# Mean and eps of the head sums on VectorE, the recurrence's elementwise chain in halves, seven temporaries

## The chip, the cores and the metric

The kernel runs on one core of one Trainium2 chip. The metric is the device time of one execution in microseconds (us). Its engines go by the profile's short names: PE is TensorE's matmul part and PEld its weight load, DVE is VectorE, ACT is ScalarE, POOL is GpSimd, and SP issues the DMAs.

## The reference

Two layers of one kind ("A": gated linear attention, grouped attention, a feed-forward part) are followed by two layers of another ("B"), on one sequence of 256 tokens of 1024 features, all in fp32. The change touches the head norms of both kinds and, in B, the gated recurrence beside the attention:

```python
for i in range(DEPTH):                                   # DEPTH = 2
    x = x + 0.5 * swiglu_ffn(rms_norm_2(x, ffn1_norm[i]), ffn1_w_in[i], ffn1_w_out[i])
    h = rms_norm_2(x, mix_norm[i])
    rx, rgate, q, k, v, f_logit, ga, gb = jnp.split(h @ w_in[i], split_idx, axis=-1)
    rx = causal_dwconv(rx, conv_w[i], conv_b[i])
    # rg_lru: r = sigmoid(rx @ w_a + b_a); ig = sigmoid(rx @ w_x + b_x)
    #   log_a = -8 * r * softplus(-lam); a = exp(log_a)
    #   u = sqrt(-expm1(2 * log_a)) * (ig * rx); y_t = a_t * y_(t-1) + u_t
    ya = (rg_lru(rx, ...) * jax.nn.gelu(rgate)) @ w_rnn_out[i]
    # q and k: rms_norm over each head of 128 features, then causal attention
    yb = forgetting_attention(q, k, v, f_logit, ...) @ w_attn_out[i]
    merged = jax.nn.sigmoid(ga + mb_a) * ya + jax.nn.sigmoid(gb + mb_b) * yb
    x = x + merged @ w_o[i]
    ...                                                  # second swiglu_ffn, gated input
```

## The kernel before

**Weights.** Every weight comes from memory once, as raw tiles of 128x1024 floats. ACT copies each tile into a rounded tile `hi` (L254) and DVE takes the rest into `lo` (L255). A product is three matmuls for each block: hi by the high part of x, hi by its low part, lo by the high part. `gemm_fm` (L292 to L294, 128x256 each) gives features by tokens, `gemm_tm` (L319 to L321, 128x512 each) tokens by features. In layer A a weight tile is split in two pieces of 128x512.

**Accumulators.** A product goes to a PSUM tile `acc` of 128x512; three buffers hold these in turn, and a buffer is free when the engine that reads the product out (ACT or DVE) has done so. A 128x512 accumulator of `gemm_fm` with 1024 input features takes 48 matmuls.

**The part of layer B around the change**, function `mixer_b`. First come the products for the recurrence's input (after the convolution `xc`, in a buffer named b3), v, f and the recurrence's output gate `rg` (buffer oh). Then small matmuls give r (b0) and ig (b1) through sigmoids with a bias (L1039), 128x256 at a time. The elementwise chain works on tiles of 128x2048: r times a factor for each feature (L1040), Tanh (L1042) and Exp (L1043) on ACT, ig times xc on POOL (L1044), a square (L1046) and a product (L1047) on DVE, a root on ACT (L1048), a product (L1049) and the recurrence itself as a scan (L1051) on DVE. The scan is one over all eight feature blocks; a memset of the first column of r (L1050) cuts them apart. The result times Gelu of rg (L1054, L1055) is split into high and low parts (L368, L369).

**Heads.** The q and k products (`heads`, four accumulators of 128x512 for q and four for k) are read out by ACT into a temporary `t` (L1064). Their squares (L471, ACT) are summed for each head (L472, DVE); `rstd` takes mean and eps (L336) and the power (L337) on POOL. DVE multiplies (L1070), PE transposes into PSUM (L1073), and ACT copies out to the q and k tiles (L1074), which take over the buffers b0 and b1 when the recurrence has no more use of them. Layer A has its own heads with the same `rstd` and a rotation behind it (L703, L712 to L724).

**Gates.** The product with w_gab follows in the same queue of PE: accumulators acc2211, acc2218, acc2225 and on in the first B layer. DVE reads each out (L383, times a row of norms) into sig_a (b2) and sig_b (b3), which are free again when the chain is through with `th` and `xc`.

**Order.** Nothing sets the order of instructions by hand. A scheduler lays out each engine's queue ahead of time from priorities: `urgent(offset, floor)` raises those of the weight splits and of the read-out of accumulators (`epilogue`). An engine takes its queue strictly in that order. Which of a pool's buffers a tile gets follows from the order in which the scheduler sees them come free. In B layers the temporaries `t` have six buffers (`T_BUFS_B`).

Of the kernel before, what the change touches and what calls it, by code (L numbers as in the profile page):

```python
# [14 lines left out]
AF = mybir.ActivationFunctionType  # L15
ALU = mybir.AluOpType
AX = mybir.AxisListType

P = 128
D = 1024  # L20
S = 256
KB = 8
HID = 2816
NHB = HID // P
EPS = 1e-6
# [5 lines left out]
SPLIT_B = 1024  # L31
EPI_PRIO = 5000
T_BUFS_A = {"t": 6, "px": 2, "sq": 2, "sy": 1, "dg": 2, "e": 1, "g": 2}
T_BUFS_B = {"t": 6, "px": 2, "sq": 1, "dg": 2}
START_PRIO = 20000
HOLD_MIX = (1, 3)
HOLD_FFN = (0, 2)
# [146 lines left out]
class Net:  # L184
# [148 lines left out]
    def rstd(self, ssq, n, cols):  # L333

        nc = self.nc
        nc.gpsimd.tensor_scalar(ssq, ssq, 1.0 / n, EPS, ALU.mult, ALU.add)  # L336
        nc.gpsimd.tensor_tensor(ssq, ssq, self.expo[:, :cols], ALU.pow)  # L337

    def rstd_of_halves(self, ssq, tag):
# [568 lines left out]
def layer_b(net, i, nrm, px, hT, following):  # L908
# [12 lines left out]
    with ExitStack() as cx:  # L921
        ms = mixer_b(net, i, cx, after)
        px = ple_input(net, a["pT_2"][i])
        nrm = NormT(net, hT, col(2))
        net.gemm_fm(ms, a["w_o"][i], net.add_scaled(hT, 1.0, nrm.blocks), tail=True)
# [20 lines left out]
def mixer_b(net, i, cx, nrm):  # L946
    nc, a, tc = net.nc, net.a, net.tc
# [3 lines left out]
    fl = lambda t: t.rearrange("p a b -> p (a b)")  # L951
# [3 lines left out]
    cc = lambda k, j: cols[:, 8 * k + j:8 * k + j + 1]  # L955
# [3 lines left out]
    sp = p1.tile([P, 16], F32, tag="sp", name=net.name("sp"))  # L959
# [41 lines left out]
    xc = big("b3")  # L1001
# [22 lines left out]
    rg = big("oh")  # L1024
# [3 lines left out]
    r, ig = big("b0"), big("b1")  # L1028
    for w, dst in ((0, r), (1, ig)):
        hi, lo = net.weight(a["rg_w"][i, w])  # L1030
        for fp in range(4):
            ps = net.pm.tile([P, 2, S], F32, tag="pm", name=net.name("rg"))
            for c in range(2):
                f = 2 * fp + c
                cs = slice(f * P, (f + 1) * P)
                nc.tensor.matmul(ps[:, c], lhsT=hi[:, cs], rhs=xch[:, f], start=True, stop=False)
                nc.tensor.matmul(ps[:, c], lhsT=hi[:, cs], rhs=xcl[:, f], start=False, stop=False)
                nc.tensor.matmul(ps[:, c], lhsT=lo[:, cs], rhs=xch[:, f], start=False, stop=True)
                nc.scalar.activation(dst[:, f], ps[:, c], AF.Sigmoid, bias=cc(5 + w, f))  # L1039
    nc.vector.tensor_tensor(r, r, sp[:, 0:8].unsqueeze(2).to_broadcast([P, KB, S]), ALU.mult)  # L1040
    th = big("b2")
    nc.scalar.activation(fl(th), fl(r), AF.Tanh)  # L1042
    nc.scalar.activation(fl(r), fl(r), AF.Exp, scale=-1.0)  # L1043
    nc.gpsimd.tensor_tensor(fl(ig), fl(ig), fl(xc), ALU.mult)  # L1044

    nc.vector.tensor_tensor(fl(xc), fl(r), fl(r), ALU.mult)  # L1046
    nc.vector.scalar_tensor_tensor(fl(th), fl(xc), 1.0, fl(th), ALU.add, ALU.mult)  # L1047
    nc.scalar.activation(fl(th), fl(th), AF.Sqrt)  # L1048
    nc.vector.tensor_tensor(fl(ig), fl(ig), fl(th), ALU.mult)  # L1049
    nc.gpsimd.memset(r[:, :, 0:1], 0.0)  # L1050
    nc.vector.tensor_tensor_scan(fl(xc), fl(r), fl(ig), 0.0, ALU.mult, ALU.add)  # L1051

    y_h, y_l = big("yh", F32R), big("yl", F32R)
    nc.scalar.activation(fl(rg), fl(rg), AF.Gelu_apprx_tanh)  # L1054
    nc.vector.tensor_tensor(fl(rg), fl(rg), fl(xc), ALU.mult)  # L1055
    for j in range(4):
        net.split_fm(blk(rg, j), y_h, y_l, 2 * j)

# [37 lines left out]
def _build(tc, a, out):  # L1096
    with ExitStack() as ctx:
# [11 lines left out]
        net.hp = hp  # L1109
        net.temporaries(ctx, T_BUFS_B)  # L1110
        net.split = SPLIT_B
# [153 lines left out]
```

## Time and profile before

| what | value |
|---|---|
| median of 3 runs | 2320.55 us (2308.11 to 2325.23) |
| profiled execution | 2315.75 us |
| span of its instructions | 2313.9 us |
| granted clock, mean | 0.991 |
| A layers, B layers | about 0 to 980 us, then to the end |
| busy: PE, DVE, ACT, POOL | 98%, 69%, 58%, 19% |

The rows below come from the profiled execution alone; 1.85 us lie around its span. "Idle before" names the engine's pause ahead of a row and what ended it. The durations of neighbouring rows of one engine overlap by about 0.1 us, so a row's share of a queue is read from its start to the next row's start.

### The profile page before, as it was taken

To read this page: it belongs to the slowest core of one execution; us is meant where nothing else is said; L and a number is where in the kernel's file an instruction comes from. 1 tells how busy PE (TensorE), PEld (TensorE's weight loads), DVE (VectorE), ACT (ScalarE), POOL (GpSimd) and SP (SyncE) were. 2 spreads that over 40 slices of the span, in tenths; PEclk is the share of its full clock that TensorE was granted. 3 is DMA by queue.
4 is the path that set the end of the run, shared out by engine and by line. 5 is a ranking of instruction groups with operands and counts; after the bars stand their busy time and mean duration, and the time that the engine had idled before them with its cause. 6 is when DMAs were issued, how large, how long until landed. Compare 5 with 4: busy or idle time off the path is not lost.

```text
span 2313.9 us, 42188 instructions
## 1 busy us (share of the span) xinstructions
PE 2262.1 (98%) x16892; PEld 2147.9 (93%) x16892; DVE 1602.1 (69%) x2133; ACT 1333.4 (58%) x2105; POOL 442.6 (19%) x443
## 2 busy tenths in 40 slices
PE   7999999998999999999999999999999999999997
PEld 6899899878899998799999899999999998999997
DVE  7876765588867765766586967655765677766655
ACT  6875554467764654554457765444644567755444
POOL 6222211063302110311001302110110104011101
PEclk9999999999999999999999999999999999999999
DMA  7445566554456666466665546666566655456663
GB/s 252 150 155 159 186 208 190 182 164 156 147 163 183 206 195 186 151 198 186 188 184 185 162 141 198 189 189 184 180 188 186 180 186 174 147 175 191 185 188 94
DMA packets 117102, 411.53 MB, mean 178 GB/s; under 512 B 14114, under 2 KB 16546, under 8 KB 116906
## 3 DMA queue, kind: packets, MB, share of 16 engines
q1 hardware_dynamic: 116906, 408.84, 57.5%
q8 instruction: 133, 2.18, 0.4%
q14 instruction: 63, 0.52, 0.1%
HBM read 407.74 MB, written 1.05 MB: 177 GB/s over the span
## 4 chain that ended last, share of the span: by engine, by line
PE 88%; DVE 4%; POOL 2%; ACT 2%; issue 2%; DMA 1%; SPq 0%; DVEq 0%; POOLq 0%; ACTq 0%
PE acc L292 22%; PE acc L293 22%; PE acc L294 22%; PE acc L319 5%; PE acc L320 5%; PE acc L321 5%; DVE lo L255 1%; ACT hi L254 1%; PE sc L586 1%; PE po L597 1%; PE gs L894 1%; POOL t L717 1%; PE sc L610 0%; POOL hg L78 0%; POOL tab L693 0%
## 5 line engine op out<-in xcount | busy, mean ns | idle before, releaser
L255 DVE TENSOR_TENSOR lo<-raw,hi 128x512 fp32r<-128x512 f32 (+1 forms) x1062 | 984.5, 954 | 424.4 <-ACT hi L254 422.4
L254 ACT ACTIVATE hi<-raw 128x512 fp32r<-128x512 f32 (+1 forms) x1062 | 824.0, 808 | 733.9 <-PE acc L293 386.3
L292 PE MATMUL acc<-xTh,hi 128*128 128x256 f32 x3296 | 923.5, 281 | 11.1 <-ACT t L1064 8.5
L293 PE MATMUL acc<-xTl,hi 128*128 128x256 f32 x3296 | 926.1, 281 | 1.0 <-DVE xTl L133 0.8
L294 PE MATMUL acc<-xTh,lo 128*128 128x256 f32 x3296 | 923.5, 280 | 0.0
L292 PEld LDWEIGHTS acc<-xTh,hi 128*128 128x128 f32 x3296 | 621.8, 189 | 13.3 <-ACT t L1064 8.9
L294 PEld LDWEIGHTS acc<-xTh,lo 128*128 128x128 f32 x3296 | 627.0, 190 | 0.4
L293 PEld LDWEIGHTS acc<-xTl,hi 128*128 128x128 f32 x3296 | 624.2, 189 | 2.8 <-DVE xTl L133 1.7
L400 POOL TENSOR_TENSOR t<-t,R 128x512 f32<-128x512 f32 x66 | 105.6, 1600 | 602.3 <-ACT t L398 602.3
L292 PE MATMUL acc<-hh,hi 128*128 128x256 f32 x704 | 197.8, 281 | 0.0
L293 PE MATMUL acc<-hl,hi 128*128 128x256 f32 x704 | 197.8, 281 | 0.0
L294 PE MATMUL acc<-hh,lo 128*128 128x256 f32 x704 | 197.8, 281 | 0.0
L319 PE MATMUL acc<-hi,xTh 128*128 128x512 f32 x416 | 164.6, 401 | 6.4 <-ACT hi L254 6.2
L320 PE MATMUL acc<-lo,xTh 128*128 128x512 f32 x416 | 166.6, 401 | 1.5 <-DVE lo L255 1.4
L321 PE MATMUL acc<-hi,xTl 128*128 128x512 f32 x416 | 165.4, 399 | 0.8 <-DVE xTl L355 0.8
L294 PEld LDWEIGHTS acc<-hh,lo 128*128 128x128 f32 x704 | 134.4, 191 | 0.0
L293 PEld LDWEIGHTS acc<-hl,hi 128*128 128x128 f32 x704 | 132.9, 189 | 0.0
L292 PEld LDWEIGHTS acc<-hh,hi 128*128 128x128 f32 x704 | 132.1, 188 | 0.0
L319 PEld LDWEIGHTS acc<-hi,xTh 128*128 128x128 f32 x416 | 79.1, 191 | 22.7 <-ACT hi L254 6.1
L320 PEld LDWEIGHTS acc<-lo,xTh 128*128 128x128 f32 x416 | 79.1, 190 | 19.0 <-DVE lo L255 3.3
L321 PEld LDWEIGHTS acc<-hi,xTl 128*128 128x128 f32 x416 | 79.2, 190 | 17.8 <-DVE xTl L355 1.5
L383 DVE TENSOR_TENSOR t<-acc,R 128x512 f32<-128x512 f32 (+1 forms) x84 | 56.8, 676 | 41.1 <-PE acc L294 41.1
(321 smaller groups left out, 3236.0 us busy)
## 6 DMA issues: line engine op xcount, KB each, us to landing
raw<-ffn_w_in SPq DMA_DIRECT2D x176, 512.0 KB, 3.7
raw<-w_ffn_in SPq DMA_DIRECT2D x88, 512.0 KB, 4.3
raw<-ffn_w_out SPq DMA_DIRECT2D x88, 512.0 KB, 4.3
raw<-w_ffn_out SPq DMA_DIRECT2D x44, 512.0 KB, 4.3
raw<-w_gate SPq DMA_DIRECT2D x32, 512.0 KB, 4.0
raw<-w_gab SPq DMA_DIRECT2D x32, 512.0 KB, 3.6
raw<-w_gqk SPq DMA_DIRECT2D x16, 512.0 KB, 3.9
raw<-w_gv SPq DMA_DIRECT2D x16, 512.0 KB, 3.3
```

The costliest lines, as they stand in the source:

```text
L254: nc.scalar.activation(hi[:, cs], raw[:, cs], AF.Copy)
L255: nc.vector.tensor_tensor(lo[:, cs], raw[:, cs], hi.bitcast(F32)[:, cs], ALU.subtract)
L292: nc.tensor.matmul(o, lhsT=hi[:, cs], rhs=xh[:, kb], start=kb == 0, stop=False)
L293: nc.tensor.matmul(o, lhsT=hi[:, cs], rhs=xl[:, kb], start=False, stop=False)
L294: nc.tensor.matmul(o, lhsT=lo[:, cs], rhs=xh[:, kb], start=False, stop=kb == nkb - 1)
L319: nc.tensor.matmul(o, lhsT=xh[:, kb, ts], rhs=hi[:, cs], start=kb == 0, stop=False)
L320: nc.tensor.matmul(o, lhsT=xh[:, kb, ts], rhs=lo[:, cs], start=False, stop=False)
L321: nc.tensor.matmul(o, lhsT=xl[:, kb, ts], rhs=hi[:, cs], start=False, stop=kb == 2 * n - 1)
L383: self.nc.vector.tensor_tensor(v(out), v(acc), r, ALU.mult)
L400: nc.gpsimd.tensor_tensor(tb, tb, nrm.R.unsqueeze(1).to_broadcast([P, 2, S]), ALU.mult)
L586: nc.tensor.matmul(sc[:, j], lhsT=q_t[:, hp * 2 + j, tt * P:(tt + 1) * P], rhs=k_t[:, hp // 2], start=True, stop=True)
L597: nc.tensor.matmul(out[:, j], lhsT=v(jt, hp // 2), rhs=p_t[:, jt], start=jt == 0, stop=jt == 1)
```

## The change

`rstd` takes the mean and eps on DVE and leaves only the power to POOL; all head norms, of A and of B, use it. The recurrence's chain is made in two halves of 128x1024 (four feature blocks each), step by step; the product ig times xc goes from POOL to DVE; the sigmoids of r and ig get the priority that read-outs have. The Gelu and the product behind the scan are in halves too. Temporaries in B layers have seven buffers.

```diff
--- before.py
+++ after.py
@@ -31,7 +31,7 @@
 SPLIT_B = 1024
 EPI_PRIO = 5000
 T_BUFS_A = {"t": 6, "px": 2, "sq": 2, "sy": 1, "dg": 2, "e": 1, "g": 2}
-T_BUFS_B = {"t": 6, "px": 2, "sq": 1, "dg": 2}
+T_BUFS_B = {"t": 7, "px": 2, "sq": 1, "dg": 2}
 START_PRIO = 20000
 HOLD_MIX = (1, 3)
 HOLD_FFN = (0, 2)
@@ -333,7 +333,7 @@
     def rstd(self, ssq, n, cols):
 
         nc = self.nc
-        nc.gpsimd.tensor_scalar(ssq, ssq, 1.0 / n, EPS, ALU.mult, ALU.add)
+        nc.vector.tensor_scalar(ssq, ssq, 1.0 / n, EPS, ALU.mult, ALU.add)
         nc.gpsimd.tensor_tensor(ssq, ssq, self.expo[:, :cols], ALU.pow)
 
     def rstd_of_halves(self, ssq, tag):
@@ -1036,23 +1036,27 @@
                 nc.tensor.matmul(ps[:, c], lhsT=hi[:, cs], rhs=xch[:, f], start=True, stop=False)
                 nc.tensor.matmul(ps[:, c], lhsT=hi[:, cs], rhs=xcl[:, f], start=False, stop=False)
                 nc.tensor.matmul(ps[:, c], lhsT=lo[:, cs], rhs=xch[:, f], start=False, stop=True)
-                nc.scalar.activation(dst[:, f], ps[:, c], AF.Sigmoid, bias=cc(5 + w, f))
-    nc.vector.tensor_tensor(r, r, sp[:, 0:8].unsqueeze(2).to_broadcast([P, KB, S]), ALU.mult)
+                with net.urgent(EPI_PRIO, 100):
+                    nc.scalar.activation(dst[:, f], ps[:, c], AF.Sigmoid, bias=cc(5 + w, f))
     th = big("b2")
-    nc.scalar.activation(fl(th), fl(r), AF.Tanh)
-    nc.scalar.activation(fl(r), fl(r), AF.Exp, scale=-1.0)
-    nc.gpsimd.tensor_tensor(fl(ig), fl(ig), fl(xc), ALU.mult)
-
-    nc.vector.tensor_tensor(fl(xc), fl(r), fl(r), ALU.mult)
-    nc.vector.scalar_tensor_tensor(fl(th), fl(xc), 1.0, fl(th), ALU.add, ALU.mult)
-    nc.scalar.activation(fl(th), fl(th), AF.Sqrt)
-    nc.vector.tensor_tensor(fl(ig), fl(ig), fl(th), ALU.mult)
-    nc.gpsimd.memset(r[:, :, 0:1], 0.0)
-    nc.vector.tensor_tensor_scan(fl(xc), fl(r), fl(ig), 0.0, ALU.mult, ALU.add)
+
+    halves = lambda step: [step(slice(4 * q, 4 * q + 4)) for q in range(2)]
+    v, s_ = nc.vector, nc.scalar
+    halves(lambda h: v.tensor_tensor(r[:, h], r[:, h], sp[:, h].unsqueeze(2).to_broadcast([P, 4, S]), ALU.mult))
+    halves(lambda h: s_.activation(fl(th[:, h]), fl(r[:, h]), AF.Tanh))
+    halves(lambda h: s_.activation(fl(r[:, h]), fl(r[:, h]), AF.Exp, scale=-1.0))
+    halves(lambda h: v.tensor_tensor(fl(ig[:, h]), fl(ig[:, h]), fl(xc[:, h]), ALU.mult))
+
+    halves(lambda h: v.tensor_tensor(fl(xc[:, h]), fl(r[:, h]), fl(r[:, h]), ALU.mult))
+    halves(lambda h: v.scalar_tensor_tensor(fl(th[:, h]), fl(xc[:, h]), 1.0, fl(th[:, h]), ALU.add, ALU.mult))
+    halves(lambda h: s_.activation(fl(th[:, h]), fl(th[:, h]), AF.Sqrt))
+    halves(lambda h: nc.gpsimd.memset(r[:, h, 0:1], 0.0))
+    halves(lambda h: v.tensor_tensor(fl(ig[:, h]), fl(ig[:, h]), fl(th[:, h]), ALU.mult))
+    halves(lambda h: v.tensor_tensor_scan(fl(xc[:, h]), fl(r[:, h]), fl(ig[:, h]), 0.0, ALU.mult, ALU.add))
 
     y_h, y_l = big("yh", F32R), big("yl", F32R)
-    nc.scalar.activation(fl(rg), fl(rg), AF.Gelu_apprx_tanh)
-    nc.vector.tensor_tensor(fl(rg), fl(rg), fl(xc), ALU.mult)
+    halves(lambda h: s_.activation(fl(rg[:, h]), fl(rg[:, h]), AF.Gelu_apprx_tanh))
+    halves(lambda h: v.tensor_tensor(fl(rg[:, h]), fl(rg[:, h]), fl(xc[:, h]), ALU.mult))
     for j in range(4):
         net.split_fm(blk(rg, j), y_h, y_l, 2 * j)
```

Line numbers behind L1039 move by up to four in the changed kernel: the head read-out L1064 becomes L1068, L1070 becomes L1074, L1051 becomes L1055, L1055 becomes L1059. Three places show what the scheduler makes of it, in the first B layer. DVE first, around the read-out of the first gate accumulator, acc2211, before:

```order
L472 TENSOR_REDUCE hss2154_14183<-sq2155_14184 128x4
L255 TENSOR_TENSOR lo2231_14548<-raw2229_14546,hi2230_14547 128x1024
L1049 TENSOR_TENSOR b12047_13685<-b12047_13685,b22062_13771 128x2048
L255 TENSOR_TENSOR lo2235_14580<-raw2233_14578,hi2234_14579 128x1024
L1070 TENSOR_TENSOR t2156_14189<-t2153_14181,hss2154_14183 128x512
L255 TENSOR_TENSOR lo2238_14610<-raw2236_14608,hi2237_14609 128x1024
L383 TENSOR_TENSOR b22209_14389<-acc2211_14391,R1686_10775 128x512
L1051 SCALAR_TENSOR_TENSOR b31945_12935<-b02046_13684,b12047_13685 128x2048
L383 TENSOR_TENSOR b22209_14389<-acc2218_14453,R1686_10775 128x512
```

And in the changed kernel:

```order
L1051 SCALAR_TENSOR_TENSOR b22062_13770<-b31945_12935,b22062_13770 128x1024
L255 TENSOR_TENSOR lo2228_14530<-raw2226_14528,hi2227_14529 128x1024
L472 TENSOR_REDUCE hss2135_14111<-sq2136_14112 128x4
L255 TENSOR_TENSOR lo2231_14560<-raw2229_14558,hi2230_14559 128x1024
L1054 TENSOR_TENSOR b12047_13685<-b12047_13685,b22062_13770 128x1024
L336 TENSOR_SCALAR hss2135_14111<-hss2135_14111 128x4
L255 TENSOR_TENSOR lo2235_14592<-raw2233_14590,hi2234_14591 128x1024
L383 TENSOR_TENSOR b22209_14401<-acc2211_14403,R1686_10775 128x512
L1055 SCALAR_TENSOR_TENSOR b31945_12935<-b02046_13684,b12047_13685 128x1024
L1074 TENSOR_TENSOR t2137_14117<-t2134_14109,hss2135_14111 128x512
```

The read-out of acc2211 (L383) stood behind the eighth lo tile of the gates (lo2238) and ahead of the whole scan. Now it stands behind the seventh (lo2235) and ahead of the scan's second half; the first half of the scan, with the Gelu product and two splits of its result, is already behind it in the queue.

PE's queue, from the last matmuls of acc2211 to the first of acc2218, with the engines that each waits for, before:

```order
L293 MATMUL acc2211_14391<-xTl1685_10774,hi2216_14423 128x256
L294 MATMUL acc2211_14391<-xTh1684_10773,lo2217_14424 128x256
L292 MATMUL acc2218_14453<-xTh1684_10773,hi2220_14455 128x256 [waits Activation_49]
L293 MATMUL acc2218_14453<-xTl1685_10774,hi2220_14455 128x256
L294 MATMUL acc2218_14453<-xTh1684_10773,lo2221_14456 128x256 [waits DVE_49]
```

And in the changed kernel:

```order
L293 MATMUL acc2211_14403<-xTl1685_10774,hi2216_14435 128x256
L294 MATMUL acc2211_14403<-xTh1684_10773,lo2217_14436 128x256
L292 MATMUL acc2218_14465<-xTh1684_10773,hi2220_14467 128x256 [waits DVE_49,PE_49]
L293 MATMUL acc2218_14465<-xTl1685_10774,hi2220_14467 128x256
L294 MATMUL acc2218_14465<-xTh1684_10773,lo2221_14468 128x256
```

The first matmul of acc2218 waited for ACT, which had its hi tile to write. It now waits for DVE and for PE itself: acc2218 lies in the buffer that acc2211 has just filled, and can start only behind its read-out by DVE. The second B layer has the same with its first two gate accumulators; no other two neighbours of the program share a buffer, and none did before.

ACT's queue, at the read-outs of the last head accumulators (acc2119, acc2142 and acc2143, whose buffers the gate product takes over; before in this order for acc2211, acc2218 and acc2225), before:

```order
L1064 ACTIVATE t2134_14097<-acc2119_14020,nr1688_10777 128x512
L254 ACTIVATE hi2216_14423<-raw2215_14422 128x1024
L471 ACTIVATE sq2136_14100<-t2134_14097 128x512
L254 ACTIVATE hi2220_14455<-raw2219_14454 128x1024
L254 ACTIVATE hi2223_14485<-raw2222_14484 128x1024
L1064 ACTIVATE t2153_14181<-acc2142_14119,nr1688_10777 128x512
L254 ACTIVATE hi2227_14517<-raw2226_14516 128x1024
L471 ACTIVATE sq2155_14184<-t2153_14181 128x512
L254 ACTIVATE hi2230_14547<-raw2229_14546 128x1024
L1048 ACT_TABLE_LOAD
L1048 ACTIVATE b22062_13771<-b22062_13771 128x2048
```

And in the changed kernel:

```order
L254 ACTIVATE hi2220_14467<-raw2219_14466 128x1024
L368 ACTIVATE yh2063_13791<-oh2017_13435 128x512
L254 ACTIVATE hi2223_14497<-raw2222_14496 128x1024
L368 ACTIVATE yh2063_13791<-oh2017_13435 128x512
L1068 ACTIVATE t2134_14109<-acc2119_14032,nr1688_10777 128x512
L254 ACTIVATE hi2227_14529<-raw2226_14528 128x1024
L471 ACTIVATE sq2136_14112<-t2134_14109 128x512
L254 ACTIVATE hi2230_14559<-raw2229_14558 128x1024
L1052 ACT_TABLE_LOAD
L1052 ACTIVATE b22062_13770<-b22062_13770 128x1024
L254 ACTIVATE hi2234_14591<-raw2233_14590 128x1024
L1068 ACTIVATE t2153_14193<-acc2142_14131,nr1688_10777 128x512
```

The read-outs of acc2119 and acc2142 stood behind weight tiles and squares alone. Now acc2119 stands behind two splits of the recurrence's result (L368), which need the first half of DVE's L1059, and acc2142 behind the second half's root (L1052). Their buffers go to acc2211 with acc2218, and to acc2225. From the first Gelu to the first gate sigmoid ACT's queue has 12 table loads in place of 7.

In the layers A the queues keep their order but for the moved L336 and some transposes of PE, which stand 7 to 11 matmuls later.

## Rows read from the trace of the kernel before

**Rows 1.** The page's head and its busy times by engine.

```profile
span 2313.9 us, 42188 instructions
...
PE 2262.1 (98%) x16892; PEld 2147.9 (93%) x16892; DVE 1602.1 (69%) x2133; ACT 1333.4 (58%) x2105; POOL 442.6 (19%) x443
```

**Rows 2.** PE's waits: line and releaser, us in total, times, longest.

```profile
PE acc L292 <- ACT t L1064: 8.5, 2, 4.3
...
PE ptq L724 <- DVE t L721: 5.8, 3, 2.7
...
PE acc L292 <- ACT t L703: 2.6, 2, 1.5
```

**Rows 3.** PE's timeline: end of acc2218, start of acc2225 (start, us, what).

```profile
1300.41 0.28 PE L294 MATMUL acc<-xTh,lo 128*128 128x256 f32 x1
1304.94 0.58 PE L292 MATMUL acc<-xTh,hi 128*128 128x256 f32 x1 [4.25 <-ACT t L1064]
```

**Rows 4.** Windows: PE, PEld, DVE, ACT, POOL busy; then clock, DMA share, GB/s.

```profile
1100.00:1150.00 50.00, 50.00 (x427) 50.00 (x427) 27.48 (x27) 22.30 (x26) 3.16 (x2) 1.00 0.63 188
1300.00:1305.00 5.00, 0.74 (x8) 0.55 (x6) 5.00 (x5) 2.97 (x5) 3.16 (x2) 0.81 0.70 205
1305.00:1310.00 5.00, 5.00 (x24) 5.00 (x25) 5.00 (x3) 2.75 (x4) 0.00 (x0) 0.51 0.62 197
```

**Rows 5.** ACT's timeline, chain and heads of the first B layer.

```profile
1239.76 1.28 ACT L1039 ACT_TABLE_LOAD   x1
1241.05 0.84 ACT L1039 ACTIVATE b<-rg,cols 128x256 f32<-128x256 f32 x2
...
1271.56 0.84 ACT L1039 ACTIVATE b<-rg,cols 128x256 f32<-128x256 f32 x2
1272.29 1.06 ACT L254 ACTIVATE hi<-raw 128x1024 fp32r<-128x1024 f32 x1
1273.24 0.69 ACT L1064 ACTIVATE t<-acc,nr 128x512 f32<-128x512 f32 x1
...
1304.20 0.69 ACT L1064 ACTIVATE t<-acc,nr 128x512 f32<-128x512 f32 x1 [1.06 <-DVE t L1070]
```

**Rows 6.** DVE's timeline, same stretch.

```profile
1283.16 5.14 DVE L1070 TENSOR_TENSOR t<-t,hss 128x512 f32<-128x512 f32 x1
...
1289.35 0.67 DVE L472 TENSOR_REDUCE hss<-sq 128x4 f32<-128x512 f32 x1
1289.95 1.21 DVE L255 TENSOR_TENSOR lo<-raw,hi 128x1024 fp32r<-128x1024 f32 x1
1291.08 2.28 DVE L1046 TENSOR_TENSOR b<-b 128x2048 f32<-128x2048 f32 x1
1293.28 1.21 DVE L255 TENSOR_TENSOR lo<-raw,hi 128x1024 fp32r<-128x1024 f32 x1
...
1303.42 0.68 DVE L1070 TENSOR_TENSOR t<-t,hss 128x512 f32<-128x512 f32 x1
...
1305.16 0.68 DVE L383 TENSOR_TENSOR b<-acc,R 128x512 f32<-128x512 f32 x1
1305.76 4.41 DVE L1051 TENSOR_TENSOR_SCAN b<-b,b 128x2048 f32<-128x2048 f32 x1
1310.09 0.66 DVE L383 TENSOR_TENSOR b<-acc,R 128x512 f32<-128x512 f32 x1
...
1325.69 0.16 DVE L569 TENSOR_SCALAR mx<-mx 128x4 f32<-128x4 f32 x1
```

**Rows 7.** POOL's timeline, same stretch.

```profile
1282.80 4.94 POOL L1044 TENSOR_TENSOR b<-b,b 128x2048 f32<-128x2048 f32 x1
1290.12 1.10 POOL L336 TENSOR_SCALAR hss<-hss 128x4 f32<-128x4 f32 x1 [2.37 <-DVE hss L472]
```

**Rows 8.** POOL's timeline, heads of the second A layer.

```profile
523.99 0.56 POOL L336 TENSOR_SCALAR hss<-hss 128x4 f32<-128x4 f32 x1 [2.01 <-DVE hss L472]
```

**Rows 9.** PE's timeline: start of acc2211.

```profile
1289.63 0.28 PE L292 MATMUL acc<-xTh,hi 128*128 128x256 f32 x1
```

## The prediction

> **What bounds the kernel now.** I read the page first: PE is busy 2262.1 of a span of 2313.9 us, DVE 69%, ACT 58%, POOL 19% [rows 1]. So all that PE ever waits is 2313.9 - 2262.1 = 51.8 us, 2.2%; beside that only a lower clock can be won back or lost. About 1% (23 us) is what a measurement of this kernel can tell from no change, and the three runs shown spread over 17 us; to pass 1% this change would have to remove nearly half of all of PE's waiting. PE's waits by releaser come second [rows 2]. Two groups belong to code that is changed: 8.5 us in two waits at L292 for ACT's head read-out L1064 (one in each B layer, the longest 4.3), and, in the A layers, 5.8 us in three waits for L721 and 2.6 us in two for L703, both behind the head norm. Third, the timeline at the first of the two long waits: acc2218's last matmul starts at 1300.41, acc2225's first only at 1304.94, after 4.25 us of idleness [rows 3]. Its cost doesn't end there: in the 5 us ahead of 1305 the granted clock is 0.81, in the next 5 us 0.51, the 1.2 GHz level, with 24 matmuls, where 117 ns each (427 in 50 us at 1.00) would have made 42.7 [rows 4]. So a pause of that length takes about (42.7 - 24) x 0.117 = 2.2 us more behind it.
>
> The cause stands in the other engines' rows. ACT's read-out at 1304.20 had waited for a buffer of t that DVE's L1070 of 1303.42 set free [rows 5, 6]. DVE works there without a pause, because it lost time at 1283.16: a head product that usually takes 0.68 us took 5.14, just as long as POOL's L1044 (1282.80, 4.94 us) was at work [rows 6, 7]. That backlog of 4.5 us is what the change takes away with POOL's product.
>
> **The change part by part.** The working unit is the distance from a row's start to the next row's, in a full queue. DVE: reduce 0.60 (1289.35 to 1289.95), lo 1.13 (to 1291.08), 2048-wide product 2.20 (to 1293.28), scan 4.33 (1305.76 to 1310.09), read-out L383 0.60 (1305.16 to 1305.76) [rows 6]. A half product has a lo tile's 1024 elements: 1.13. Half a scan: 2.2. A head product or a 512-wide split is taken like L383's 512 elements: 0.6. ACT: hi tile 0.95 (1272.29 to 1273.24), a pair of sigmoids 0.73 (1271.56 to 1272.29), table load 1.29 (1239.76 to 1241.05) [rows 5]; a 1024-wide step 0.95, a 512-wide one 0.57, near half of that plus a little.
>
> *Mean and eps on DVE.* POOL takes 0.56 us in A and up to 1.10 in B [rows 7, 8]. The row nearest to the new instruction is DVE's tensor_scalar on 128x4, 0.16 us [rows 6], about 0.13 in a queue. DVE's hand-over to POOL remains, since the power stays there. So a step of the head chain gets 0.65 - 0.13 = 0.5 us shorter. In A this chain is what PE waits for, at five waits [rows 2]: 5 x 0.5 = -2.6 us. Bounds: 0, if the weight splits queued on DVE eat it; -4.7, if the 0.95 us of the longer POOL rows goes at each. In B, sixteen such instructions put 16 x 0.13 = 2 us on DVE, counted below where they stand.
>
> *Seven temporaries.* The wait at 1304.20 for a buffer goes, but ACT's row ahead of it ended at 1304.20 - 1.06 = 1303.14, so alone this is worth about 1 us in each B layer. It is contained in the walk below.
>
> *The chain in halves, up to the sigmoids of ig.* ACT's new queue from the first sigmoids' table load to the sigmoid that completes the first half of ig holds 7 loads, 9 hi tiles, 12 sigmoids, 5 steps of 1024, 3 read-outs and 3 squares: 9.0 + 8.6 + 4.4 + 4.8 + 3.4 = 30.2 us. From 1239.76, and with some 2 us of waiting for PE's products, that is 1272, which is where the old kernel had its fourth pair (1272.29). The two loads more in this stretch cost nothing, since two 2048-wide steps (Tanh, Exp) are half done later; cover gone, they cost 2.6. Ends: 2 us either way.
>
> *DVE from there to the read-out of acc2211.* From the first product of ig (start about 1272.5) DVE's new queue holds 9 half products (10.2 us), 11 lo (12.4), half a scan (2.2), 3 reduces (1.8), 3 head products (1.8), 2 splits (1.2), 3 tensor_scalars (0.4) and the read-out itself (0.6): 30.6 us, so 1303.1. In the old trace that read-out starts at 1305.16 and ends at 1305.84 [rows 6]. The 4.5 us of POOL's block are gone, but the product of ig (2 x 1.13), half a Gelu product, two splits and the tensor_scalars now stand ahead of it, and that is most of it.
>
> *The accumulators' buffers, which decide.* In the old order acc2211, acc2218 and acc2225 took three buffers, and nobody waited for the read-out of acc2211 at 1305. In the new order acc2218 has the buffer of acc2211. First, acc2211 itself: its buffer is that of acc2119, which ACT now reads out behind two splits that wait for DVE's first L1059. Six half products, five lo, half a scan, two reduces, two head products and a tensor_scalar are 17.2 us, so L1059 ends at 1289.8; then two splits, a hi tile and the read-out on ACT make 2.8 with a hand-over: acc2211 starts at 1292.8, where it started at 1289.63 [rows 9]. Its 48 matmuls (5.6 us) end at 1298.4, and PE stands until DVE's read-out at about 1303.4, 5 us, in which the clock falls as it did before [rows 4]. Then acc2218's 48 matmuls and two head transposes that moved ahead of its end take 6.5: acc2225 starts at 1309.9, against 1304.94 [rows 3], 5.0 later. Of this 0.9 is transposes done earlier. Behind it the last transposes of k stand behind ACT's copies, which come after a root's and the gate's table load: I take 1 us, between 0 and those two loads, 2.6. Sum +5.1 us in a B layer, less the seven-buffer gain, which is already in it as no read-out in the walk waits for t. The half-clock stretch behind the pause occurs in both kernels and cancels. Two layers: +10.2. The second layer's trace has the same block on DVE and the same sharing.
>
> The sum: 2315.75 (profiled; span 2313.9 and 1.85 around it) + 10.2 - 2.6 = 2323.4. The profiled execution is 4.8 us under the median of the three runs; 2323 is 0.3% over it and 0.1% over that median. I give 2323.
>
> *A rule that speaks against the halves.* In the old trace a load takes 1.28 us and the next activation starts 0.01 us behind it [rows 5]. The Trainium skill, ScalarE: Activation LUTs, section What ACT_TABLE_LOAD costs, gives about 1283 ns for the load, which this trace shows, and a drain of about 1380 ns beside it, 2.66 us for a switch, which these rows don't show. Five more loads in a layer would by that page be an estimated 13.3 us of ACT in place of 6.4. While the loads stay off the path the sum is the same by both; on it, the last rival says what each gives.
>
> **The rivals.** *DVE is in time (faster).* If ACT finds less to wait for than in the old trace (its waits shrink and DVE begins the half chain earlier), the read-out of acc2211 comes right after its last matmul. Then each B layer loses the wait of 4.25 but for the 0.9 of a read-out, and the slow stretch of 2.2: 2 x (-3.35 - 2.2) - 2.6 = -13.7, 2302. For it: POOL's block on DVE is gone, and a head product then costs 0.68. Against: the read-out would have to come some 8 us earlier than the count of DVE's queue allows.
>
> *One wait takes the other's place (no change).* The pause at acc2218 is as long as the old one at acc2225; what is left is A's -2.6: 2313. For it: the count has an uncertainty of some 4 us, and the pause absorbs just that. Against: acc2211's late start adds to it.
>
> *ACT becomes late (slower).* Five more table loads, 5 x 1.29 = 6.4 us in each B layer, come on the path if ACT reaches the two splits ahead of acc2119's read-out later than DVE's L1059 ends (1289.8). From 1272.3 ACT has there a read-out, 6 hi tiles, two squares, two loads and so on, some 14 us, that is 1286.4: a margin of 3.4. If its waits for PE and DVE in that stretch pass 3.4 us, each load counts, and the second pause has its own slow stretch: 2 x (6.4 + 2.2) = 17.2 more than forecast, 2341. For it: the head read-outs now wait for a chain that crosses DVE and ACT several times. With the drain that the Trainium skill, ScalarE: Activation LUTs, section What ACT_TABLE_LOAD costs, adds to a load, it would be an estimated 2355.
>
> **How the numbers follow.** The forecast has 0.45, no change 0.22, faster 0.15, slower 0.18. The range goes from 2300 to 2341: the lower end lets in most of the faster rival, the upper one half of the slower, and the bounds of the single terms (2 us in ACT's stretch, 0 to 2.6 behind k, 0 to -4.7 in A) lie inside it. Faster by over 1% means under 2297.3: 0.06, from the edge of the faster rival. Slower by over 1% means above 2343.8: 0.09, half of the slower one. The rest, 0.85, is within 1%.
>
> **What would show it.** In the changed kernel's waits, L1064's (now L1068's) 8.5 us at L292 should be gone or small, and a wait at L292 for DVE's L383 of some 5 us should stand in each B layer, with a granted clock near 0.5 behind it, and one of 3 us ahead of it for ACT. DVE's head products should all take 0.7 us, none 5. In A the waits for L721 and L703 should lose 2.6 of 8.4. If there is no wait for L383, the buffer step is wrong; if ACT's splits wait for nothing and still come after 1290, the table loads are the cause. I am wrong altogether if PE's time moves elsewhere than in A's heads and B's mixer.

## The result

The changed kernel took 2340.49 us (median of 6 runs, 2333.86 to 2345.46), the kernel before 2316.37 us in the same comparison: a ratio of 1.0098, with a 95% interval of 1.0068 to 1.0127. It is slower by about 1%. Forecast was 2323, with a range from 2300 to 2341.

The page of the changed kernel answers to [rows 1]: the span is 25.8 us longer in the profiled execution (2341.44 us against 2315.75), and PE's waiting in it has grown from 51.8 to 67.6 us.

```profile
span 2339.7 us, 42231 instructions
...
PE 2272.1 (97%) x16892; PEld 2153.3 (92%) x16892; DVE 1607.6 (69%) x2181; ACT 1357.2 (58%) x2129; POOL 406.9 (17%) x411
```

PE's waits (line and releaser, us in total, times, longest) answer to [rows 2]:

```profile
PE acc L292 <- DVE b L383: 7.9, 2, 4.3
PE ptq L724 <- DVE t L721: 7.9, 6, 2.6
PE acc L292 <- ACT t L1068: 7.6, 2, 3.8
...
PE ptp L593 <- ACT hi L254: 2.9, 3, 2.5
...
PE acc L292 <- ACT t L703: 2.5, 2, 1.5
```

The wait for L383 that the prediction named is there, 4 us in each B layer. So is the one for ACT's read-out (L1064, now L1068) ahead of it, at acc2211, for which the prediction's last part has 3 us: it is 3.8. L724's wait for L721, which was to shrink, has grown from 5.8 to 7.9 us, in six waits instead of three. The total alone shows little: a second trace of the kernel before (run 9) has 9.2 us in eight. Its place tells more. In the first A mixer it is 3.8 us, where the first trace of before has none and run 9 has 1.5; in the second A layer it is 4.0 in place of 5.8. L593's (transposes in the A layers' attention), 0.2 us in the old trace, is new.

To see where the time goes, the start of each of the 16,892 matmuls is set against that of the matmul with the same number in the trace of before (a matmul's place in the order differs by less than a hundred). Stretches: the first A mixer, the rest up to the recurrence (A layers and the first feed-forward product of B), the first B mixer from the recurrence on, then up to the next, the second, and the end. The last column tells what part of the difference lies in the plain distance of matmuls in a long product (about 113 or 118 ns from one start to the next in either trace), of which more below; the column ahead of it holds all the rest.

| matmuls | before, us | changed: waits and clock | changed: distance |
|---|---|---|---|
| 0 to 1200, first A mixer | 197.0 | +10.7 | +0.2 |
| to 8400 | 1027.3 | -2.3 | 0.0 |
| to 9600, first B mixer | 170.4 | +8.0 | +0.7 |
| to 13500 | 468.1 | 0.0 | 0.0 |
| to 14700, second B mixer | 174.0 | +7.5 | +0.6 |
| to the end | 264.0 | 0.0 | 0.0 |

So the loss has two places: the first A mixer, for which -1 us was forecast (its two of the five waits), and the two B mixers, +5.1 each in the forecast.

**First A mixer.** PE's timeline (start, us, what, idle before) has pauses ahead of transposes that the old trace has not, of the heads (L724) and of the attention (L593):

```profile
54.17 0.63 PE L724 MATMUL ptq<-ident,t 128*128 128x128 f32 x4 [1.22 <-DVE t L721]
55.85 0.38 PE L292 MATMUL acc<-xTh,hi 128*128 128x256 f32 x1 [1.05 <-ACT t L703]
...
61.82 1.09 PE L724 MATMUL ptq<-ident,t 128*128 128x128 f32 x4 [2.62 <-DVE t L721]
...
101.35 0.84 PE L593 MATMUL ptp<-ident,t 128*128 128x128 f32 x6 [2.48 <-ACT hi L254]
```

DVE and POOL in front of the pause at 61.82:

```profile
53.95 0.68 DVE L472 TENSOR_REDUCE hss<-sq 128x4 f32<-128x512 f32 x1
54.54 1.28 DVE L255 TENSOR_TENSOR lo<-raw,hi 128x512 fp32r<-128x512 f32 x2
55.74 0.16 DVE L336 TENSOR_SCALAR hss<-hss 128x4 f32<-128x4 f32 x1
55.81 1.28 DVE L255 TENSOR_TENSOR lo<-raw,hi 128x512 fp32r<-128x512 f32 x2
57.99 0.69 DVE L712 TENSOR_TENSOR t<-t,hss 128x512 f32<-128x512 f32 x1 [0.90 <-POOL hss L337]
...
60.98 0.69 DVE L721 TENSOR_TENSOR t<-t,t 128x512 f32<-128x512 f32 x1 [0.83 <-POOL t L717]
```

```profile
55.98 1.98 POOL L337 TENSOR_TENSOR hss<-hss,expo 128x4 f32<-128x4 f32 x1 [3.11 <-DVE hss L336]
58.83 2.12 POOL L717 TENSOR_TENSOR t<-t,tab 128x128 f32<-128x128 f32 x4 [0.87 <-PE acc L293]
```

The sum (L472) ends at 54.63. The scheduler puts two weight splits (L255) behind it, and the mean and eps (L336) only starts at 55.74, 1.11 us later, although it takes 0.16. Then POOL's power takes 1.98 us while DVE is busy. From the end of the sum to that of the power it is 3.33 us. In the old trace the same head group took 2.33: the sum ended at 50.37, and POOL's own step came 0.22 us later.

```profile
49.69 0.68 DVE L472 TENSOR_REDUCE hss<-sq 128x4 f32<-128x512 f32 x1
...
50.59 0.69 POOL L336 TENSOR_SCALAR hss<-hss 128x4 f32<-128x4 f32 x1
51.37 1.33 POOL L337 TENSOR_TENSOR hss<-hss,expo 128x4 f32<-128x4 f32 x1
```

Over the six head groups of this layer the way from sum to power is 14.9 us, in this trace and in that of the step on VectorE alone (below), against 10.9 before. Behind the pause of 2.62 us the granted clock is lower (0.68 of full in its 5 us), and behind the second, of 2.48 at 101.35, once more (0.78): by the trace's clock records each has a stretch of 3.41 us at 1.2 GHz behind it. That doesn't come with every such pause: in the second trace of the changed kernel (run 10) PE waits 2.54 us at the same place, and the clock stays at 1.00 in these 5 us. Windows (PE, PEld, DVE, ACT, POOL busy; clock, DMA share, GB/s):

```profile
60.00:65.00 5.00, 3.18 (x15) 3.21 (x16) 3.18 (x8) 2.40 (x5) 3.78 (x9) 0.68 0.10 42
100.00:105.00 5.00, 3.65 (x15) 3.06 (x16) 5.00 (x12) 5.00 (x11) 0.00 (x0) 0.78 0.33 104
1300.00:1305.00 5.00, 1.56 (x10) 1.56 (x11) 4.76 (x6) 4.14 (x6) 4.09 (x1) 0.93 0.46 151
1305.00:1310.00 5.00, 5.00 (x34) 5.00 (x33) 4.34 (x5) 2.00 (x2) 0.68 (x2) 0.73 0.60 183
1315.00:1320.00 5.00, 4.82 (x22) 4.85 (x23) 4.62 (x6) 4.28 (x7) 0.53 (x2) 0.50 0.47 167
```

The first window in run 10:

```profile
60.00:65.00 5.00, 2.41 (x20) 2.28 (x21) 3.45 (x9) 2.47 (x6) 3.78 (x10) 1.00 0.15 59
```

What PE waits in this stretch has grown from 12.4 to 18.7 us, and two stretches at half clock cost 3.4 more: 9.7 of the 10.7. In run 10 it is 20.3 us of waiting and 1.7 of slow clock, for the same loss. Followed matmul by matmul, the first trace loses 1.2 us ahead of the first head transposes, 4.2 at the head transposes, 3.8 at the pause of L593 and 1.8 behind it. The first 1.2 are start-up scatter: traces with the old rstd in A have -0.3 to +1.9 there.

**B mixers.** PE's timeline answers to [rows 3, 9]; all of it is 8.9 us later by what came before:

```profile
1303.44 0.38 PE L292 MATMUL acc<-xTh,hi 128*128 128x256 f32 x1 [3.82 <-ACT t L1068]
...
1315.18 0.55 PE L292 MATMUL acc<-xTh,hi 128*128 128x256 f32 x1 [4.29 <-DVE b L383]
```

ACT reads acc2119 out behind two splits, the first of which waited for DVE's L1059; DVE's own rows from the first product of ig to the read-out of acc2211 answer to [rows 6]:

```profile
1300.72 0.63 ACT L368 ACTIVATE yh<-oh 128x512 fp32r<-128x512 f32 x1 [4.20 <-DVE oh L1059]
...
1302.72 0.67 ACT L1068 ACTIVATE t<-acc,nr 128x512 f32<-128x512 f32 x1
```

```profile
1282.47 1.23 DVE L1048 TENSOR_TENSOR b<-b,b 128x1024 f32<-128x1024 f32 x1 [0.64 <-ACT b L1040]
...
1292.68 0.69 DVE L1074 TENSOR_TENSOR t<-t,hss 128x512 f32<-128x512 f32 x1 [0.90 <-POOL hss L337]
...
1299.47 1.22 DVE L1059 TENSOR_TENSOR oh<-oh,b 128x1024 f32<-128x1024 f32 x1
...
1301.81 1.22 DVE L1050 TENSOR_TENSOR b<-b 128x1024 f32<-128x1024 f32 x1
1302.94 1.22 DVE L255 TENSOR_TENSOR lo<-raw,hi 128x1024 fp32r<-128x1024 f32 x1
...
1305.66 0.69 DVE L1074 TENSOR_TENSOR t<-t,hss 128x512 f32<-128x512 f32 x1 [0.90 <-POOL hss L337]
...
1314.35 0.68 DVE L383 TENSOR_TENSOR b<-acc,R 128x512 f32<-128x512 f32 x1
```

Counted: the first product of ig starts at 1282.47 (forecast 1272.5 + 8.9 = 1281.4), L1059 ends at 1300.69 (1298.7), acc2211 starts at 1303.44 (1301.7), the read-out ends at 1315.03 (1312.3). The order of events is the one forecast; each step is 1 to 3 us late. The two waits of 0.90 are for POOL's power, which took 3.04 and 4.72 us here with DVE busy, in place of 1.01 at 1281.91, when DVE had little to do:

```profile
1289.60 3.04 POOL L337 TENSOR_TENSOR hss<-hss,expo 128x4 f32<-128x4 f32 x1 [3.94 <-DVE hss L336]
1300.91 4.72 POOL L337 TENSOR_TENSOR hss<-hss,expo 128x4 f32<-128x4 f32 x1 [8.27 <-DVE hss L336]
```

PE's waits in the two stretches grow from 4.3 and 4.2 us to 9.0 and 8.7, and what the half clock costs on top by 2.3 and 1.8: 7.0 and 6.3 of the 8.0 and 7.5. Of the loss 7.3 and 6.8 us are there when the third gate accumulator is under way. The changed kernel has nine more table loads than before in each of these stretches, not five; the other four stand in the attention behind that place. A half product takes 1.13 to the next row (1301.81 to 1302.94), as costed.

### The profile page after: what moved, and what is told of

It reads as the page before. It is cut to its first block, busy times and chain, and to the rows that moved or that the text cites. A ratio compares the mean times of both kernels' runs of the same rounds, so it can differ in the third digit from the quotient of the medians.

```text
span 2339.7 us, 42231 instructions
## 1 busy us (share of the span) xinstructions
PE 2272.1 (97%) x16892; PEld 2153.3 (92%) x16892; DVE 1607.6 (69%) x2181; ACT 1357.2 (58%) x2129; POOL 406.9 (17%) x411
## 4 chain that ended last, share of the span: by engine, by line
PE 84%; DVE 5%; ACT 4%; POOL 3%; issue 2%; DMA 1%; SPq 0%; DVEq 0%; POOLq 0%; ACTq 0%
PE acc L292 22%; PE acc L293 22%; PE acc L294 22%; PE acc L320 5%; PE acc L319 5%; PE acc L321 5%; DVE lo L255 1%; ACT hi L254 1%; POOL t L717 1%; POOL hss L337 1%; PE po L597 1%; PE gs L894 1%; PE sc L586 0%; PE sc L610 0%; POOL hg L78 0%
## 5 line engine op out<-in xcount | busy, mean ns | idle before, releaser
L255 DVE TENSOR_TENSOR lo<-raw,hi 128x512 fp32r<-128x512 f32 (+1 forms) x1062 | 986.6, 955 | 435.1 <-ACT hi L254 433.1
L337 POOL TENSOR_TENSOR hss<-hss,expo 128x4 f32<-128x4 f32 (+1 forms) x28 | 48.3, 1724 | 263.1 <-DVE hss L336 260.4
```

The source lines that it names most:

```text
L255: nc.vector.tensor_tensor(lo[:, cs], raw[:, cs], hi.bitcast(F32)[:, cs], ALU.subtract)
```

## The experiments

Each run states its ratio to the kernel before, with the 95% interval, and the waits-and-clock part of its trace by stretch (first A mixer; to matmul 8400; first B mixer; second B mixer). Theory 1 has the loss of the B layers come from the shared buffer and that of the first A mixer from the moved step; theory 2 has the B layers lose by the halves themselves.

**1. The step on VectorE alone** (kernel before).

```diff
 def rstd(self, ssq, n, cols):
...
-        nc.gpsimd.tensor_scalar(ssq, ssq, 1.0 / n, EPS, ALU.mult, ALU.add)
+        nc.vector.tensor_scalar(ssq, ssq, 1.0 / n, EPS, ALU.mult, ALU.add)
```

> The kernel before with the mean and eps on VectorE alone (whole chain, six temporaries). Theory 1 (the loss in the first A layer is made by this edit, through the queues): about +9 us, of that some +11 in the first A layer with waits of TensorE at L724 for L721, -1.5 in the second, and nothing in the B layers, where the waits for L1064 stay. Rival (that loss is start-up scatter of the DMAs): the first A layer as before, the whole within 3 us of before.

0.9972 (0.9958 to 0.9985): 2312.6 us. Stretches: +9.2; -0.7; -0.1; -0.8. The first A mixer loses nearly what it loses in the changed kernel, and nothing else does. The total misses the expectation of +9: its trace has +7.9 us by waits and clock, yet the median of the timed runs is 6 us under the kernel before. Its traced execution is the slowest of its twelve (2320.79). So the loss by the step shows in the stretches of the trace and not in the time of this run. PE's waits:

```profile
PE acc L292 <- ACT t L1064: 8.8, 2, 4.4
PE ptq L724 <- DVE t L721: 6.6, 6, 2.1
...
PE ptp L593 <- DVE t L574: 2.8, 1, 2.8
```

**2. The halves alone** (the changed kernel with this undone):

```diff
-T_BUFS_B = {"t": 7, "px": 2, "sq": 1, "dg": 2}
+T_BUFS_B = {"t": 6, "px": 2, "sq": 1, "dg": 2}
...
-        nc.vector.tensor_scalar(ssq, ssq, 1.0 / n, EPS, ALU.mult, ALU.add)
+        nc.gpsimd.tensor_scalar(ssq, ssq, 1.0 / n, EPS, ALU.mult, ALU.add)
```

> The chain in halves with its priorities alone; mean and eps on GpSimd, six temporaries. Here acc2211, acc2218 lie in different buffers. Theory 1 (the B layers lose by the shared buffer): no wait for L383, A layers as before, each B layer between -6 and +2 us, so 2304 to 2320. Theory 2 (they lose by the halves themselves, by table loads and the chain's crossings between ScalarE and VectorE): about +8 us in each B layer, 2333.

1.0062 (1.0046 to 1.0079), 2333.72 us. Stretches: +0.4; +1.4; +6.1; +8.2. On its face this speaks for theory 2. But the trace still has the wait for L383 that the expectation denied:

```profile
PE acc L292 <- DVE b L383: 7.8, 2, 4.6
...
PE acc L292 <- ACT t L1068: 5.3, 2, 2.7
```

Here acc2225, the third gate accumulator, was given acc2211's buffer; acc2218 was not. That wasn't seen when the expectation was written. PE also waits 3.5 us for transposes of B's attention (L625; 1.2 in the changed kernel), behind the accumulators. The run doesn't tell the theories apart; run 5 does.

**3. A buffer of its own for acc2218** (changed kernel; `gemm_fm` takes the accumulator pair `own` from the norms' PSUM pool):

```diff
+                if b // 2 == own:
+                    acc = self.pg.tile([P, 512], F32, tag="pg", name=self.name("acc"))
+                else:
                     acc = self.ps.tile([P, 512], F32, tag="acc", name=self.name("acc"))
...
-    net.gemm_fm(xs, a["w_gab"][i], e_gate)
+    net.gemm_fm(xs, a["w_gab"][i], e_gate, own=1)
```

> The changed kernel with the second gate accumulator (acc2218 and its like in the second B layer) in the PSUM buffer that norms use, which is free there, so that it shares none with acc2211. Theory 1: the wait for L383 (4 us in each B layer) and half-speed clock behind it go, the wait for ScalarE's read-out of some 3.8 us ahead stays: 8 to 12 us under the changed kernel, 2328 to 2332. Theory 2: the wait moves to the next accumulator, and the time stays within 3 us of 2340.

1.0039 (1.0026 to 1.0052), 2327.78 us. Stretches: +9.6; +1.5; -0.4; +0.9. No wait for L383 is left, the one for ACT's read-out stays at 7.2 us, and both B mixers are back at the time of before. Theory 1 holds, theory 2 falls. The first A mixer keeps its loss. The time against the changed kernel falls by 12.7 us; by waits and clock its trace has 12 us less than that kernel's, by distance another 7.

```profile
PE acc L295 <- ACT t L1071: 7.2, 2, 3.6
```

**4. The step on GpSimd in the A layers only** (changed kernel; a flag, set in `mixer_b`, chooses the engine):

```diff
-        nc.vector.tensor_scalar(ssq, ssq, 1.0 / n, EPS, ALU.mult, ALU.add)
+        (nc.vector if self.in_b == True else nc.gpsimd).tensor_scalar(ssq, ssq, 1.0 / n, EPS, ALU.mult, ALU.add)
```

> The changed kernel with the mean and eps on GpSimd in the A layers and on VectorE in the B layers only; the shared buffer is there. Theory 1: the first A layer is as before (0 for +11), B as in the changed kernel (+17 in both): about 2332. Rival (start-up scatter): as the changed kernel, 2340.

1.0095 (1.0081 to 1.0109), 2341.56 us. Stretches: +0.8; -0.2; +9.1; +10.7. The first A mixer's loss is gone with the step, so it isn't scatter. The total misses the expected 2332 and is no lower than the changed kernel's. In the trace the B mixers lose 4.3 us more than there, with the same two accumulators in one buffer; most of that is PE's wait at transposes of B's attention, 4.5 us in place of 1.2:

```profile
PE ptp L626 <- ACT hi L255: 4.5, 3, 1.8
```

**5. Halves and seven temporaries** (changed kernel, the step back on GpSimd as in run 2, seven kept).

> The changed kernel with the mean and eps back on GpSimd: halves, priorities and seven temporaries. Here the gate accumulators take three buffers in turn (in the run with halves alone the third had the first one's). Theory 1 (a shared buffer makes the loss in B): no wait for L383, A as before, each B layer within 2 us of before, so 2315 to 2322. Theory 2 (the halves themselves): +6 to +8 us in each B layer, 2331 to 2335.

0.9942 (0.9920 to 0.9964), 2308.93 us. Stretches: +1.5; -0.8; +0.1; -0.1. The accumulators take three buffers in turn, no wait for L383 is among PE's waits, and the halves, with their five more table loads in each layer, cost nothing in B:

```profile
PE ptq L724 <- DVE t L721: 7.0, 6, 2.9
PE acc L319 <- ACT hi L254: 6.3, 2, 5.8
PE acc L292 <- ACT t L1068: 4.9, 2, 2.6
```

The wait for ACT's read-out is 4.9 us in place of 8.5 [rows 2]; it now stands at the second gate accumulator. Nothing is the net: PE's waits and the slow clock are 1.0 to 1.5 us less than before in each B mixer, so a loss of that size in each goes unexplained.

**6. Seven temporaries alone** (`T_BUFS_B` of the kernel before: 6 to 7).

> The kernel before with seven temporaries in the B layers alone. Both theories: ScalarE reaches the read-out some 1 us earlier, so the wait of 4.3 us at L292 for L1064 falls to about 3.3, twice: -2 us, hardly to be told from before.

0.9932 (0.9908 to 0.9957), 2302.49 us, where a gain of 2 us was expected. Stretches: +1.9; +1.3; -1.6; -0.6. By waits and clock the size expected in B is met, but not the way: the wait for L1064 didn't fall to 3.3, it is gone, and PE waits at the k transposes instead. The trace has another 13.5 us by distance.

```profile
PE ptq L1073 <- ACT b L1074: 4.9, 2, 2.4
```

**7. No step at all** (kernel before; a 129th column of the squares holds eps):

```diff
-        sq = self.t(tag="sq")[:, :nh * P]
-        nc.scalar.activation(sq, acc, AF.Square)
+        sq = self.t((P, 4, P + 1), tag="sq")[:, :nh]
+        nc.gpsimd.memset(sq[:, :, P:], EPS)
+        nc.scalar.activation(sq[:, :, :P], acc.rearrange("p (h d) -> p h d", h=nh), AF.Square, scale=P ** -0.5)
...
-        self.rstd(ssq, P, nh)
+        nc.gpsimd.tensor_tensor(ssq, ssq, self.expo[:, :nh], ALU.pow)
```

> The kernel before without any step for mean and eps: ScalarE's square is scaled, and the sum by VectorE runs over a 129th column that holds eps (set by GpSimd ahead of time); the power follows on GpSimd at once. Queues of TensorE nearly as before. Theory 1a (in the first A layer the step on VectorE stands behind weight splits and lengthens the chain): with the step gone the chain is 0.6 us shorter for each head group, the first A layer loses nothing or gains up to 3 us. Theory 1b (any shorter step makes the scheduler move transposes forward, and TensorE waits): a loss of several us there as with the step on VectorE.

0.9975 (0.9960 to 0.9990), 2312.84 us. Stretches: +2.1; +5.4; -0.1; -1.1, and +4.5 in the feed-forward parts between and behind. These +4.5, and 1 us of the +5.4, aren't waiting: PE waits as long as before in those parts, and some 1,700 matmuls of this trace stand 120 to 124 ns apart (89 in the first trace of before), which the split into two distances doesn't take in. The first A mixer doesn't lose the 9 us, as 1a says; but it doesn't gain either, although the way from sum to power is 7.0 us over its six groups (10.9 before). PE waits 1.5 us for L721's like there (3.8 in the changed kernel). For theory 1b the run says less than was meant: it moved the last three groups of head transposes in that layer by -1, +5 and 0 matmuls, and the attention's not at all. It is the second A layer where the attention's transposes stand 21 to 47 matmuls earlier, about as in the first layer of the changed kernel; PE waits 0.8 us ahead of them there, and the stretch of the attention loses some 3 us.

**8. A buffer of its own for acc2225, kernel before** (as run 3, `own=2`).

> The kernel before, with the third gate accumulator (acc2225 and its like) in the PSUM buffer that norms use. If the 4.25 us wait for the read-out of acc2143 and the slow clock behind it cost what the trace of before says, it gains 4.25 + 2 to 3.4 us in each B layer: 12 to 15 us under before, 2304 to 2307. Rival: TensorE waits for the next accumulator, or for the k transposes, instead: no change.

0.9927 (0.9902 to 0.9952), 2300.89 us: even under the 2304 to 2307 expected, but not by the expected way. Stretches: +0.9; +0.2; -2.6; -2.7. The 8.5 us for L1064 are gone, and the rival came in part: PE waits 5.7 us at the k transposes for ACT's copies. Distance gives the other 13.2 us of the trace.

```profile
PE ptq L1076 <- ACT b L1077: 5.7, 2, 2.8
```

**9 and 10. Both kernels once more, unchanged**, one profiled execution each.

> The kernel before once more, unchanged, to see whether the distance of its matmuls in long products (113 or 118 ns in the traces so far) belongs to the program or to the execution. If to the program: 118 ns again in the two feed-forward products after the recurrence of each B layer, time 2314 to 2322. If to the execution: another pattern, and a time that differs by about 7 us for each product.

> The changed kernel once more, unchanged: the waits of its first trace (7.9 us for L383, 7.9 us for L721) and its lower-clock stretches near 62, 103, 1304, 1314, 1973 and 1987 us should come again, whichever theory holds of their cause; the matmul distance as in its first trace if that belongs to the program. 2335 to 2345.

Run 9 (2326.57 us, above the expected 2314 to 2322): waits and clock +1.2 in all, distance +9.4, nearly all of it in two stretches of the A layers; in the feed-forward products of B it is as in the first trace. Run 10 (2343.11 us): stretches +10.9; -0.7; +7.0; +8.6, distance +1.6. The loss repeats place by place. Of the six slow stretches that were to come again, the one near 62 us didn't.

**11 and 12. Combinations.** Run 11 is run 8 with seven temporaries, run 12 is run 5 with acc2225's own buffer.

> The kernel before with the third gate accumulator in the norms' buffer and seven temporaries: both runs that gained in one. If the gains of these two came from the waits (2.6 and 1 us in a B layer) they add up to a few us under the one of them alone, 2297 to 2302; if they came from the distance of the matmuls, no sum is due, 2298 to 2312.

> The changed kernel with mean and eps on GpSimd and the third gate accumulator in the norms' buffer: halves, priorities, seven temporaries. The read-out wait of 4.9 us for L1068 that the run without the extra buffer kept should go: 3 to 5 us under it, 2303 to 2307, if no other wait takes its place (rival: the k transposes wait for ScalarE's copies, 2309 as it was).

Run 11: 0.9943 (0.9922 to 0.9964), 2304.81; the gains don't add (stretches in B -0.4 and -0.7). Run 12: 1.0001 (0.9987 to 1.0016), 2320.62, far from the 2303 to 2309 of its expectation: waits as in run 5 (4.7 us for the read-out of ACT), distance +9.8 where run 5 had -19.3. The buffer couldn't remove that wait, because it stands at the second gate accumulator, in run 5 too, and the third was given the buffer. Runs 5, 6, 8 and 11 beat both kernels, the one before by 0.6 to 0.7%, runs 1 and 7 by 0.3%; of that waits and clock explain 4 us at most.

## Why the prediction came out as it did

- **Bound by PE's waits, under 1% to move: right, but barely.** The ratio is 1.0098 and its interval goes to 1.0127. The time is inside the range, at its upper end, 17 us over the value given. That it lies inside is luck: the upper end, 2341, was taken from a rival whose mechanism did not occur, while two terms of the sum were off the same way, the one in A by its sign and the one in B by its size.
- **Mean and eps on DVE, -2.6 us in A: wrong, the step that failed.** It cost +8.4 us in the A layers (+10.7 and -2.3) of the trace; the first A mixer has it in all four traces with the step in A (runs 1, 3 and 10 too, +9.2 to +10.9), and runs 2, 4, 5, 6 and 8 show its absence without (+0.4 to +1.9). The -2.3 is no sure gain: run 10 has -0.7 there. The timed runs don't show the cost by themselves, since run 1 is faster than before and run 4 no faster than the changed kernel. The working took 0.13 us for the instruction and let it start at once. On DVE's queue two weight splits stood between the sum and it, and POOL's power beside the busy DVE took longer, so the chain grew by 4.0 us over the first layer's six groups instead of shrinking by 0.5 each. The bound "0, if the weight splits eat it" named the cause and denied it a loss: it took the time hidden in the split for the most that could go, without the pauses of PE and the lower clock that can stand behind them (two pauses of 2.5 us, each with 3.41 us at half; in run 10 one of the two). Run 7, with no step at all, loses 2.1 us there, so a loss of this size doesn't come from any shorter chain as such. How much comes from the longer chain and how much from PE's moved queue wasn't separated: every run that loses here has both.
- **The order in A: misread.** The text ahead of the prediction says that A's queues keep their order but for transposes that stand 7 to 11 matmuls later. That holds for the second A layer. In the first the last three groups of transposes stand 5, 18 and 27 matmuls earlier, and those of the attention 14 to 47. That the scheduler does so because it expects a short step on DVE is likely, but no run shows its reason.
- **Seven temporaries, about 1 us in each B layer: right** in size (run 6: 1.6 and 0.6), not in the way: there the wait for ACT's read-out goes altogether, and 2.4 us at the k transposes take its place.
- **ACT's stretch up to ig costs nothing: nearly right.** The first product of ig starts 1.1 us later than the count.
- **acc2218 in acc2211's buffer, +5.1 us in each B layer: right in mechanism, too small.** Runs 3 and 5 take the sharing away in two ways, and B is back within 1 us of before in both; run 4 has it and run 2 the like for the third accumulator, and both lose. Measured are +8.0 and +7.5. Missing are, first, a second slow stretch: the 3.82 us pause ahead of acc2211 has 3.41 us at half clock behind it, the one ahead of acc2218 another 6.83, where before had 6.83 behind its one pause; "occurs in both kernels and cancels" counted one. It is worth 2.3 and 1.8 us. Second, the queue's own lateness of 1 to 3 us, from two waits of DVE of 0.90 for POOL's power, and the 1.1 above. The working also makes 1292.8 of 1289.8 and 2.8, which is 1292.6; nothing hangs on that.
- **The rivals.** "ACT becomes late" gave 2341, the measured time, but not its mechanism: ACT waited 4.20 us for L1059 before the split, so the table loads stayed off the path, and run 5 has the five more at no net loss. "DVE is in time" and "one wait takes the other's place" did not occur. The drain that the Trainium skill, ScalarE: Activation LUTs, section What ACT_TABLE_LOAD costs, puts beside a load doesn't show in the changed kernel's rows either: a load at 1280.31 takes 1.28 us, and the next sigmoid starts at 1281.60.
- **The 4.25 us wait and the slow clock behind it as the price to win back: overrated.** Run 8 removes the wait and most of the slow clock and gets 2.6 us in each B layer; the k transposes wait instead.

## What to carry to other kernels

An operation moved to a faster engine is as fast as its place in that engine's queue: look up what the scheduler puts between it and its input, and price the pause of the engine that waits at the end together with the slow clock that can stand behind it. An accumulator's buffer is part of the critical path: after any edit, list which accumulators share one with a near predecessor, at every distance up to the number of buffers, since an order that looks better may have put two neighbours into one. And take each stretch's difference from the traces before believing a total: here totals moved by as much without a wait.

## What the runs showed of the hardware

Matmuls of a long product mostly keep one of two distances from start to start at a granted clock of 1.00 (run 7 has some between 120 and 124 ns too). Windows of the same feed-forward stretch, of the kernel before and of run 6:

```profile
1500.00:1550.00 50.00, 50.00 (x427) 50.00 (x426) 30.36 (x31) 23.25 (x27) 8.38 (x5) 1.00 0.63 192
2150.00:2200.00 50.00, 50.00 (x427) 50.00 (x426) 30.68 (x31) 23.16 (x27) 7.92 (x5) 1.00 0.61 189
```

```profile
1500.00:1550.00 50.00, 50.00 (x444) 50.00 (x443) 31.78 (x33) 25.15 (x29) 8.52 (x5) 1.00 0.63 197
2150.00:2200.00 50.00, 50.00 (x443) 50.00 (x442) 31.97 (x33) 24.82 (x29) 7.07 (x4) 1.00 0.64 193
```

427 in 50 us are 117 ns each, 444 are 113, for the same instructions. In the stretch around 1430 us where the two traces part, the distance changes only at the few small matmuls of the norm (L156, L163), and then stays for the product. One feed-forward product in B is 6.8 us longer or shorter by it. Twice the kernel before gave the same distance there, and so did twice the changed one, while two stretches of the A layers differed between executions of the same kernel by 4.7 and 4.9 us. In the traces this is most of the gain of runs 5, 6, 8 and 11; that it is also the gain of run 1, whose traced execution has little of it (2.9 us), is argued and not shown. Between the traces of the kernel before and the changed one it makes 1.5 us, so it isn't the cause of the result. What sets it stays open.
